# A ring of their own for the norms' small tiles, and 32-byte steps between operand slots, in a hybrid streaming block on one core

## The chip, the cores and the metric

The kernel runs on one core of a Trainium2 chip. The metric is the device time of one execution in microseconds (us); for the kernel before it is 1710.43 us, the median of three runs (1708.87 to 1712.0).

A core has a matrix engine (TensorE, PE; its weight loads appear as a row of their own, PEld), VectorE (DVE), ScalarE (ACT) and GpSimd (POOL), each of which works through its own list of instructions in order, and DMA queues that SyncE (SP), ACT or POOL issue to.

## The reference

One layer takes x (1024 frames of 1024 channels) and 256 memory tokens. Everything is float32.

```python
h = _rmsnorm(x, norm_mix_g[l])
z = h @ w_in[l]
(hq, hf, hi, hg, fq, fk, fv, ff, mq, gate_logits) = jnp.split(z, pts, axis=-1)
y_a = _hgrn2_mixer(hq, hf, hi, hg, lower_bounds[l], hgrn_norm_g[l])
y_b = _fox_mixer(fq, fk, fv, ff, fox_f_bias[l], fox_q_norm_g[l], fox_k_norm_g[l])
mem_kv = _rmsnorm(mem, norm_mem_g[l]) @ mem_kv_w[l]
y_c = _memory_mixer(mq, mem_kv, mem_q_norm_g[l], mem_k_norm_g[l])
gates = jax.nn.sigmoid(gate_logits).reshape(B, T, N_BRANCH, D_MODEL)
merged = sum over branches of gates[:, :, b] * (y_b @ w_br_b)
x = x + merged @ w_out[l]
h2 = _rmsnorm(x, norm_ffn_g[l])
x = x + _conv_glu_ffn(h2, ffn_w_up[l], ffn_conv_w[l], ffn_conv_b[l], ffn_w_down[l])
```

(The two lines on the branches are drawn together here.) The memory mixer normalises its queries and keys per head, takes a softmax over the 256 tokens for each of four heads, and sums the values. The forgetting attention (FoX) normalises its queries and keys per head of 64 channels too. `_rmsnorm` divides by the root of the mean square. Such a division per head is what the kernel calls a head norm.

## The kernel before, in words

**Products.** Each float32 operand is kept as a high and a low part, and `mm3` (lines 122 to 124) makes a product of three matmuls: high by high, high by low, low by high. The large products use seven products of sums of blocks in place of eight (a Strassen-like scheme). The blocks of x are the *families* B11, B21, T2, T1, T3, B22 and T4, each with a high and a low tile of 8 KB per partition in the pool `pfam`; the weights' parts are split on the fly into the slots `wh` and `wl`. A family or slot is read again and again by PE.

**Stages.** By the time of the trace: up to 40 us the memory's keys and values and the loading of x; to 305 us the dense stage, in five units (0: memory queries, 1: HGRN's values, 2: FoX queries and keys of the first half, 3: FoX values, 4: FoX queries and keys of the second half); to 960 us the gates, HGRN, FoX and the branches; to 1070 us the out projection; to 1490 us the way up; then the way down. A unit of the dense stage (`tm_unit`) makes its seven products one after the other, each in two banks of PSUM (`pp`, `lg` or `po`), and hands each finished quarter to a `put` function.

**The head norm** (`head_norm`, lines 601 to 612) is called for the quarters of units 0, 2 and 4: ACT squares the quarter into the two banks of a product (L608), DVE sums the squares per head into a small tile `r` (L609), `rstd_small` scales it on DVE (L140) and raises it to the power of -1/2 on POOL (L141), and DVE multiplies the quarter `e` by it (L612). PE then turns the quarter with an identity into the same two banks (L617), from where ACT and DVE split it. Until that is done, these two banks cannot take a later product; the next unit's first product, with B11, needs the pair of unit 2's second norm.

**The memory attention** (`mem_attn`) is woven into the dense stage: eight times a load and twice two steps. *Logits*: six matmuls, DVE's maximum (L667) into a small tile `mst`, its negation (L668), exponentials on ACT (L670), the reciprocal on DVE (L672), the scaling on POOL (L674). *Values*: four turnings on PE (L682), the split of the result into `mph` on ACT (L128) and `mpl` on DVE (L136), six matmuls, and a copy on ACT (L690). Each step's PSUM tile is one of the two `tr` banks. `stage` takes three such steps from the list after each product of a unit.

**Small tiles.** `small` hands out slots of one ring of eight, 64 bytes per partition each. Both `r` of a head norm (named `r2` or `r4`) and `mst` come from it, in the order in which the program allocates them. A new tile of a ring waits for the tile that had its slot before.

**The order of the work** on each engine is not written out by hand: the program is emitted in the order of the code, and a scheduler that simulates the engines picks from it, at build time, the order that each engine's list gets. Which tile waits for which slot is part of what it reckons with. The chip then runs these lists as they stand.

**Addresses.** Tiles are placed one after the other in their pools. `EDGE` and `BASE` are the lengths (in floats) of two unused tiles ahead of the others on the two sides of the memory. Before the change, all families and all slots of the weights' parts start at a multiple of 128 bytes.

Of the kernel before, what the change touches and what calls it, by code (L numbers as in the profile page):

```python
# [9 lines left out]
F32 = mybir.dt.float32  # L10
F32R = mybir.dt.float32r
# [4 lines left out]
P = 128  # L16
T = 1024
D = 1024
KC = D // P
HB = 512  # L20
# [16 lines left out]
UNITS = [[("f", 0), ("q", 0)], [("g", 0), ("f", 1)], [("q", 1), ("g", 1)], [("f", 2), ("q", 2)],  # L37
         [("g", 2), ("f", 3)], [("q", 3), ("g", 3)]]
UNITS += [[("gt", i), ("gt", i + 1)] for i in range(0, 24, 2)]
EDGE, BASE = 120, 56  # L40
TMIN, TMAX = -(1.0 - 2.0 ** -24), 1.0 - 2.0 ** -23


# [26 lines left out]
def tile_block(ctx: ExitStack, tc: tile.TileContext, xT, x_rows, memT, mem_rows, vec, fbias, mats, hmask, w_ff, w_tm, w_cm,  # L70
# [4 lines left out]
    cp = ctx.enter_context(tc.tile_pool(name="cp", bufs=1))  # L75
# [22 lines left out]
    lbm, lbe0, lbe1 = (cp.tile([P, 4], F32, tag=t, name=t) for t in ("lbm", "lbe0", "lbe1"))  # L98

    def small(name, w):  # L100
        return cp.tile([P, 16], F32, tag="small", name=name, bufs=8)[:, :w]

    edge = ctx.enter_context(tc.tile_pool(name="edge", bufs=1, side="right"))
    edge.tile([P, EDGE], F32, tag="edge", name="edge")
# [2 lines left out]
    def col(i):  # L107
        return cv[:, i:i + 1]
# [29 lines left out]
    def rstd_small(out, ss, n):  # L138
        w = ss.shape[1]
        V.tensor_scalar(out, ss, 1.0 / n, EPS, ALU.mult, ALU.add)  # L140
        return G.tensor_tensor(out, out, mhalf[:, :w], ALU.pow)  # L141
# [23 lines left out]
    pfam = tc.alloc_tile_pool(name="pfam", bufs=1, side="right", reuse_waits="tile")  # L165
    fam = {}

    def fam_tile(name, part, shape=(P, 4, HB), dt=F32R):
        return pfam.tile(list(shape), dt, tag=f"{name}{part}", name=f"{name}{part}")

    rp = tc.alloc_tile_pool(name="rp", bufs=1, side="left", reuse_waits="tile")
    xp = tc.alloc_tile_pool(name="xp", bufs=1, side="left", reuse_waits="tile")
    for name in ("B11", "B21"):
        fam[name] = [fam_tile(name, p) for p in "hl"]

    def raw_tile(name="raw"):
# [3 lines left out]
        return rp.tile([P, T], dt, tag="ws", name=name, bufs=2)  # L180

    def parts_tiles():
        return [rp.tile([P, T], F32R, tag=t, name=t, bufs=3) for t in ("wh", "wl")]

    def e_tile(name="e"):
        return rp.tile([P, 4, 256], F32, tag="e", name=name, bufs=3)
# [1 line left out]
    def ko_tile(name="ko", dt=F32R):  # L188
        return rp.tile([P, 2, HB], dt, tag="ko", name=name, bufs=2)

    xr = [fam_tile(f, p, (P, 2, T), F32) for f in ("T2", "T1") for p in "hl"]
    mt = fam_tile("T3", "h", (P, KC, NM), F32)
    mem_row = fam_tile("T3", "l", (P, 2, T), F32)
    umh = fam_tile("T4", "h", (P, KC, NM))
    uml = fam_tile("T4", "l", (P, KC, NM))
    xq = [[xp.tile([P, 4, HB], F32, tag=f"x{c}{n}", name=f"x{c}{n}") for n in range(2)] for c in range(2)]
# [85 lines left out]
    def kv_chunk(q):  # L282

        ps = pairs[2 * (q // 4)]
        h, l = parts_tiles()
        for i in range(2 if q == 0 else 1):
            sl = slice(i * HB, (i + 1) * HB) if q == 0 else slice(0, T)
            split(S, h[:, sl], l[:, sl], wkv[q][:, sl])
        h, l = (t.rearrange("p (a b) -> p a b", a=2) for t in (h, l))
        for kk in range(2):  # L290
            k = 2 * (q % 4) + kk
            for m in range(2):
                ms = slice(m * P, (m + 1) * P)
                mm3(ps[m], umh[:, k, ms], uml[:, k, ms], h[:, kk, :], l[:, kk, :], k == 0, k == KC - 1)
# [49 lines left out]
    def quarter(c, n, k):  # L344
        return xq[c][n][:, k, :]

    def turn_x(c, n, k):
        ps = ps_tr()
        for b in range(4):
            PE.transpose(ps[:, b * P:(b + 1) * P], x_row(4 * n + b)[:, (4 * c + k) * P:(4 * c + k + 1) * P], ident)  # L350
        S.activation(quarter(c, n, k), ps, AF.Copy, scale=col(C_GX + 4 * c + k))
# [10 lines left out]
    def new_family(name):  # L362
        fam[name] = [fam_tile(name, p) for p in "hl"]

    def family_block(name, k, src, sub=None):
        h, l = fam[name]
        split(S, h[:, k, :], l[:, k, :], src, sub)
# [30 lines left out]

    def second_half():
        fam["B12"] = [fam_tile("T4", p) for p in "hl"]  # L400
        new_family("B22")
        for c, name in enumerate(("B12", "B22")):
            for k in range(4):
                turn_x(c, 1, k)
                family_block(name, k, quarter(c, 1, k))
# [30 lines left out]
    def tm_operand(src):  # L436
        h, l = parts_tiles()
        split(S, h, l, src)
        return [t.rearrange("p (k c) -> p k c", k=4) for t in (h, l)]
# [129 lines left out]
    def forget_row():  # L569
        fb = small("fb", 2)[:16, :]  # L570
        V.memset(fb, 0.0)
        a, b = (half_tile(f"fr{i}")[:16, :] for i in range(2))
        for n in range(2):
            SP.dma_start(fb[8 * n:8 * n + 8, 0:1], fbias)
            SP.dma_start(a[8 * n:8 * n + 8, :], ffd[:, n * HB:(n + 1) * HB])
        V.tensor_scalar(a, a, fb[:, 0:1], None, ALU.add)
        S.activation(b, a, AF.Abs)
        S.activation(b, b, AF.Sigmoid)
        S.activation(b, b, AF.Ln)
        V.scalar_tensor_tensor(out=b, in0=a, scalar=0.0, in1=b, op0=ALU.min, op1=ALU.add)  # L580
        V.tensor_tensor_scan(a, ones[:16, :].to_broadcast([16, HB]), b, 0.0, ALU.mult, ALU.subtract)
        SP.dma_start(fb[8:16, 1:2], a[0:8, HB - 1:HB])
        V.tensor_scalar(a, a, fb[:, 1:2], None, ALU.add)
        for n in range(2):
            SP.dma_start(negFd[:, n * HB:(n + 1) * HB], a[8 * n:8 * n + 8, :])
# [15 lines left out]
    def head_norm(z, nh, bank):  # L601

        zz = [z[:, 2 * b:2 * b + 2, :].rearrange("p b (h d) -> p (b h) d", h=nh) for b in range(2)]
        r = small(f"r{nh}", 4 * nh)
        rs = [r[:, 2 * nh * b:2 * nh * (b + 1)] for b in range(2)]
        for b in range(2):
            sq = bank[b].rearrange("p (c d) -> p c d", c=2 * nh)
            S.activation(sq, zz[b], AF.Square)  # L608
            V.reduce_sum(rs[b], sq, axis=AX.X)  # L609
        rstd_small(r, r, 256 // nh)  # L610
        for b in range(2):
            V.tensor_mul(zz[b], zz[b], rs[b].unsqueeze(2).to_broadcast([P, 2 * nh, 256 // nh]))  # L612
# [37 lines left out]
    def mem_attn(h, n):  # L650
# [8 lines left out]
        def logits(j):  # L659
            mqh, mql = tiles  # L660
            ps = ps_tr()
            pt = half_tile("mpt").rearrange("p (b m) -> p b m", b=2)
            st = small("mst", 8)
            for b in range(2):
                tsl = slice((2 * j + b) * P, (2 * j + b + 1) * P)
                mm3(ps[:, b * NM:(b + 1) * NM], mqh[:, tsl], mql[:, tsl], mem["mkh"][:, h, :], mem["mkl"][:, h, :], True, True)
            V.reduce_max(st[:, 0:2], ps.rearrange("p (b m) -> p b m", b=2), axis=AX.X)  # L667
            V.tensor_scalar(st[:, 2:4], st[:, 0:2], -1.0, None, ALU.mult)  # L668
            for b in range(2):
                S.activation(pt[:, b, :], ps[:, b * NM:(b + 1) * NM], AF.Exp, bias=st[:, 2 + b:3 + b],  # L670
                             accum_out=st[:, 4 + b:5 + b])
            V.reciprocal(st[:, 6:8], st[:, 4:6])  # L672
            for b in range(2):
                G.tensor_scalar(pt[:, b, :], pt[:, b, :], st[:, 6 + b:7 + b], 0.0, ALU.mult, ALU.add)  # L674
            pts.append(pt)
# [26 lines left out]
    def mem_steps():  # L702
# [9 lines left out]
        slow.extend(steps)  # L712

    stage(0, put_mq, (None, second_half, None, differences, mem_keys, third))
    small_consts()
    stage(1, put_hi, (last, mem_steps, forget_logits, forget_row))
# [513 lines left out]
    wp = tc.alloc_tile_pool(name="wp", bufs=1, side="left", reuse_waits="tile")  # L1230
    pr = tc.alloc_tile_pool(name="pr", bufs=1, side="right", reuse_waits="tile")
    r2 = pr.tile([P, T], F32, tag="r2", name="r2")
    pl = tc.alloc_tile_pool(name="pl", bufs=1, side="right", reuse_waits="tile")
# [8 lines left out]
        return wp.tile([P, 2, HB], F32, tag="raw", name=name, bufs=4)  # L1242

    def part_tiles(bufs=4):
        return [wp.tile([P, 2, HB], F32R, tag=t, name=t, bufs=bufs) for t in ("wh", "wl")]

    def w_operand(src):
        parts = []
# [93 lines left out]
            G.dma_start(b11, b21, accum_op=ALU.add)  # L1342

    def operand_parts(h, src):
        l = pl.tile([P, HB], F32R, tag="wl2", name="wl2", bufs=5)
        late["cast"] = S.copy(h, src)  # L1346
        late["split"] = V.tensor_sub(l, src, h.bitcast(F32))  # L1347
        return h, l

    def first_operands(a11, s1, s2, s4):  # L1350

        (h0, _), (h1, _) = part_tiles(), part_tiles()
        o1 = operand_parts(h0[:, 0, :], a11)
        o2 = operand_parts(h0[:, 1, :], s1)
        o3 = operand_parts(h1[:, 0, :], s2)
        return o1, o2, o3, operand_parts(pl.tile([P, HB], F32R, tag="wl2", name="wh2", bufs=5), s4)

    with tc.issue_after(marks["last"].ins):
        run_all(up_sums())
# [9 lines left out]
    for i, (c, n, mine, first, sign, last) in enumerate((  # L1369
# [11 lines left out]
        if i < 6:  # L1381
            ops.append(operands(i + 1))
        else:
            begun = first_operands(*first_raw)
# [53 lines left out]
    pw = tc.alloc_tile_pool(name="pw", bufs=1, side="left", reuse_waits="tile")  # L1438

    def operand(src):  # L1440
        return operand_parts(pw.tile([P, HB], F32R, tag="wh2", name="wh2", bufs=6), src)

    def sum_of(i, a, b):
        t = pw.tile([P, HB], F32, tag=f"s{i}", name=f"s{i}")
# [99 lines left out]
    for p in range(NF // 2):  # L1544
# [32 lines left out]
        for i in range(2):  # L1577
            f = 2 * p + i
            c = pq.tile([P, T], F32, tag="fc", name="fc", bufs=4)
            w = [col(C_CW + t * NF + f) for t in range(3)]  # L1580
# [88 lines left out]
    for a, b, own, first, c, n, sign, last, xq in (  # L1669
# [9 lines left out]
        for i, ks in enumerate(steps):  # L1679
# [11 lines left out]
            for m in range(4):  # L1691
                w = 256 if end and ks.stop == NP and m == 3 else HB
# [115 lines left out]
```

## Time and profile before

| | |
|---|---|
| median of three runs | 1710.43 us (1708.87 to 1712.0) |
| the profiled execution's own time | 1705.72 us |
| its span in the trace | 1704.0 us |
| instructions | 24944 |
| PE busy | 1660.5 us, 97% of the span |
| DVE, ACT, POOL busy | 1211.0, 844.3, 452.7 us |
| moved by DMA | 305.54 MB |

Rows of a stage (view of windows) give its bounds in us, its length, and then for each engine the busy time and the number of instructions (x), the granted clock of PE as a share of full speed, the DMA engines' mean busy share, and GB/s. Rows of the timeline give the start, the duration, engine, line, operation and tiles (out<-in); what stands in brackets is the idle time just before and what ended it. Rows of waits give the engine, what it was about to do, what it waited for, the total, the number of times and the longest. Rows of groups give the busy time and the mean duration in ns, then the idle time ahead of them.

### The profile page before, as it was taken

What the parts mean: (1) busy time and instruction counts of PE and PEld (TensorE: products, weight loads), DVE (VectorE), ACT (ScalarE), POOL (GpSimd) and SP (SyncE); (2) the same over time, 40 slices, a digit from 0 to 9 for tenths busy, and PEclk for the clock granted to TensorE, in tenths of its full rate; (3) what the DMA queues carried; (4) which work ended last, traced back from release to release, by engine and by line L of the source; (5) the groups of instructions that cost most, each with busy time, mean ns of one, the idle gap of its engine ahead of it and who ended that gap; (6) DMA issues with size and microseconds to landing.
All of it is one profiled execution on the core that took longest, in us unless ns stands there. A gap on an engine that the chain in (4) does not pass through costs nothing. (4 is left out here: it accounts for less than half of the span.)

```text
span 1704.0 us, 24944 instructions
## 1 busy us (share of the span) xinstructions
PE 1660.5 (97%) x8883; PEld 1417.7 (83%) x8883; DVE 1211.0 (71%) x2177; ACT 844.3 (50%) x1449; POOL 452.7 (27%) x482
## 2 busy tenths in 40 slices
PE   7999989999999999999999999999999999999999
PEld 5989979977788888888888788788888888888887
DVE  7874565668787676698766767787778878765654
ACT  7745544456666666556432356643434434343432
POOL 1433344365544444323011133311111111100000
PEclk9999989999999999999999999999999999999999
DMA  7352343365564444455966998866445445394772
GB/s 288 110 187 96 108 136 147 125 200 167 174 192 138 146 141 148 161 167 191 317 194 174 300 264 207 227 177 172 153 134 140 118 146 152 117 397 158 246 272 87
DMA packets 134749, 305.54 MB, mean 179 GB/s; under 512 B 14328, under 2 KB 31992, under 8 KB 133984
## 3 DMA queue, kind: packets, MB, share of 16 engines
q1 hardware_dynamic: 101008, 210.87, 36.5%
q0 software_dynamic: 24400, 78.39, 18.3%
q10 hardware_dynamic: 9216, 14.68, 2.3%
q8 instruction: 70, 1.15, 0.3%
q14 instruction: 55, 0.45, 0.1%
HBM read 223.21 MB, written 107.41 MB: 194 GB/s over the span
## 5 line engine op out<-in xcount | busy, mean ns | idle before, releaser
L1346 ACT CAST wh<-s 128x512 fp32r<-128x512 f32 x80 | 48.8, 619 | 113.2 <-PE pp L123 61.1
L128 ACT CAST dwh<-wr 128x1024 fp32r<-128x1024 f32 (+1 forms) x41 | 40.2, 980 | 115.7 <-PE tr L123 39.2
L730 ACT CAST uh<-ur 128x512 fp32r<-128x512 f32 x78 | 48.2, 618 | 77.5 <-PE pp L123 70.9
L1346 ACT CAST wh<-rw 128x512 fp32r<-128x512 f32 x70 | 43.0, 620 | 84.0 <-PE pp L123 45.5
L1470 POOL DMA_DIRECT2D rw<-in_w_up x40 | 22.3, 567 | 188.4 <-DVE wl L1347 142.4
L1045 POOL TENSOR_SCALAR pt<-pt,st 128x128 f32<-128x128 f32 (+3 forms) x64 | 56.8, 889 | 56.8 <-DVE st L1044 38.2
L136 DVE TENSOR_TENSOR dwl<-wr,dwh 128x1024 fp32r<-128x1024 f32 (+1 forms) x41 | 46.3, 1129 | 34.1 <-ACT dwh L128 33.3
L122 PE MATMUL pp<-B21h,uh 128*128 128x512 f32 x168 | 66.8, 400 | 3.8 <-DVE gt L895 2.6
L731 DVE TENSOR_TENSOR ul<-us,uh 128x512 fp32r<-128x512 f32 x72 | 55.2, 770 | 20.1 <-ACT uh L730 19.5
L1043 ACT ACTIVATE pt<-pt,st 128x128 f32<-128x128 f32 (+3 forms) x64 | 49.8, 778 | 39.1 <-DVE st L1040 33.6
L736 POOL TENSOR_TENSOR us<-ur 128x512 f32<-128x512 f32 x36 | 48.6, 1351 | 71.5 <-DMA ur<-in_w_cm 55.4
L731 DVE TENSOR_TENSOR ul<-ur,uh 128x512 fp32r<-128x512 f32 x78 | 60.8, 779 | 8.8 <-ACT uh L730 8.3
L124 PE MATMUL pp<-B21h,ul 128*128 128x512 f32 x168 | 66.3, 394 | 0.1
L123 PE MATMUL pp<-T2l,uh 128*128 128x512 f32 x168 | 66.3, 395 | 0.0
L122 PE MATMUL pp<-T2h,uh 128*128 128x512 f32 x168 | 66.2, 397 | 0.0
L123 PE MATMUL pp<-B21l,uh 128*128 128x512 f32 x168 | 66.0, 393 | 0.0
L124 PE MATMUL pp<-T2h,ul 128*128 128x512 f32 x168 | 65.9, 393 | 0.0
L736 POOL TENSOR_TENSOR us<-us,ur 128x512 f32<-128x512 f32 x36 | 50.7, 1409 | 38.1 <-issue 31.9
L730 ACT CAST uh<-us 128x512 fp32r<-128x512 f32 x72 | 43.9, 615 | 33.7 <-POOL us L736 17.9
L1347 DVE TENSOR_TENSOR wl<-rw,wh 128x512 fp32r<-128x512 f32 x70 | 47.0, 685 | 17.7 <-PE pp L124 14.9
L136 DVE TENSOR_TENSOR wl<-raw,wh 128x1024 fp32r<-128x1024 f32 x29 | 36.8, 1273 | 27.7 <-ACT wh L128 27.5
L1347 DVE TENSOR_TENSOR wl<-s,wh 128x512 fp32r<-128x512 f32 x80 | 54.5, 681 | 0.0
(721 smaller groups left out, 6157.6 us busy)
## 6 DMA issues: line engine op xcount, KB each, us to landing
rw<-in_w_up POOLq DMA_DIRECT2D x40, 512.0 KB, 4.8
ur<-in_w_cm SPq DMA_DIRECT2D x72, 256.0 KB, 3.5
sd<-in_w_dn POOLq DMA_DIRECT2D x30, 512.0 KB, 6.1
br<-yd SPq DMA_DIRECT2D x30, 512.0 KB, 4.6
gd<-uo ACTq DMA_DIRECT2D x48, 256.0 KB, 2.2
gt<-gd SPq DMA_DIRECT2D x48, 256.0 KB, 7.5
yd<-fc SPq DMA_DIRECT2D x44, 256.0 KB, 2.0
raw<-in_w_tm SPq DMA_DIRECT2D x20, 512.0 KB, 3.4
```

Of the source, the lines that this page charges most:

```text
L122: PE.matmul(ps, lh, rh, start=first, stop=False, skip_group_check=more)
L123: PE.matmul(ps, lh, rl, start=False, stop=False, skip_group_check=more)
L124: return PE.matmul(ps, ll, rh, start=False, stop=last, skip_group_check=more)
L128: S.copy(out, in_)
L136: return (sub or V).tensor_sub(l, src, h.bitcast(F32))
L730: marks["cast"] = S.copy(h, src)
L731: V.tensor_sub(l, src, h.bitcast(F32))
L736: G.tensor_add(t, a, b)
L1043: S.activation(pt[:, :ns], pt[:, :ns], AF.Exp, bias=st[:, 2:3], accum_out=st[:, 3:4])
L1045: G.tensor_scalar(pt[:, :ns], pt[:, :ns], st[:, 3:4], 0.0, ALU.mult, ALU.add)
L1346: late["cast"] = S.copy(h, src)
L1347: late["split"] = V.tensor_sub(l, src, h.bitcast(F32))
```

## The change

It has two parts.

*Two rings.* The slots of `small` shrink from 64 to 32 bytes, still eight of them; `head_norm` takes its `r` from a new ring, `norm`, with four slots of 64 bytes. Together they take the same 512 bytes.

*Addresses.* Unused tiles of 32 bytes (`gap`) go ahead of the families B21, T2, T1, T3, T4 and B22, and the first unused tile on that side (`EDGE`) is 256 bytes shorter. The slots `wh`/`wl` of the dense stage and of the out projection and `wl2`/`wh2` of the way up become 32 bytes longer than what is used of them, so that the slots of one ring stand 32 bytes further apart. By the addresses of the built kernels, the families start after the change at 64 (B11), 96 (B21), 0 (T2), 32 (T1), 64 (T3), 96 (T4) and 0 (B22) within 128 bytes; the dense stage's `wh` at 0, 32 and 64 and its `wl` at 96, 0 and 32; those of the out projection and the way up in like steps of 32. The gates' slots `uh` and `ul` all move to 64. The way down's slots stay at multiples of 128.

```diff
-EDGE, BASE = 120, 56
+EDGE, BASE = 56, 56
...
     def small(name, w):
-        return cp.tile([P, 16], F32, tag="small", name=name, bufs=8)[:, :w]
+        return cp.tile([P, 8], F32, tag="small", name=name, bufs=8)[:, :w]
...
+    def gap(name):
+        pfam.tile([P, 8], F32, tag=f"gap{name}", name=f"gap{name}")
+
     for name in ("B11", "B21"):
+        if name == "B21":
+            gap(name)
         fam[name] = [fam_tile(name, p) for p in "hl"]
...
-        return [rp.tile([P, T], F32R, tag=t, name=t, bufs=3) for t in ("wh", "wl")]
+        return [rp.tile([P, T + 8], F32R, tag=t, name=t, bufs=3)[:, :T] for t in ("wh", "wl")]
...
-    xr = [fam_tile(f, p, (P, 2, T), F32) for f in ("T2", "T1") for p in "hl"]
+    xr = []
+    for f in ("T2", "T1"):
+        gap(f)
+        xr += [fam_tile(f, p, (P, 2, T), F32) for p in "hl"]
+    gap("T3")
...
+    gap("T4")
...
         fam["B12"] = [fam_tile("T4", p) for p in "hl"]
+        gap("B22")
         new_family("B22")
...
     def head_norm(z, nh, bank):
...
-        r = small(f"r{nh}", 4 * nh)
+        r = cp.tile([P, 16], F32, tag="norm", name=f"r{nh}", bufs=4)[:, :4 * nh]
...
     def part_tiles(bufs=4):
-        return [wp.tile([P, 2, HB], F32R, tag=t, name=t, bufs=bufs) for t in ("wh", "wl")]
+        return [wp.tile([P, T + 8], F32R, tag=t, name=t, bufs=bufs)[:, :T].rearrange("p (a b) -> p a b", a=2) for t in ("wh", "wl")]
...
     def operand_parts(h, src):
-        l = pl.tile([P, HB], F32R, tag="wl2", name="wl2", bufs=5)
+        l = pl.tile([P, HB + 8], F32R, tag="wl2", name="wl2", bufs=5)[:, :HB]
```

(`wh2` is lengthened in the same way at its two places.) Lines behind the first added ones have numbers higher by up to 12 in the kernel after: L609 becomes L621, L612 L624, L617 L629, L667 L679, L674 L686, L682 L694.

The number of instructions of each engine stays the same. Their order changes in the units 2 to 4 of the dense stage alone.

On DVE, around the second head norm of unit 2, the order before is this (`e_2307` is the quarter, `r4_2423` its small tile, `mst` the small tiles of the attention; the numbers tell one tile from another):

```order
L667 TENSOR_REDUCE mst_2359<-tr_2357 128x2
L609 TENSOR_REDUCE r4_2423<-pp_201 128x8
L609 TENSOR_REDUCE r4_2423<-pp_202 128x8
L668 TENSOR_SCALAR mst_2359<-mst_2359 128x2
L136 TENSOR_TENSOR mpl_2462<-tr_2456,mph_2461 128x512
L140 TENSOR_SCALAR r4_2423<-r4_2423 128x16
L672 RECIPROCAL mst_2359<-mst_2359 128x2
L612 TENSOR_TENSOR e_2307<-e_2307,r4_2423 128x512 x2
```

And after the change, where the same quarter is `e_2313` and its small tile `r4_2429`:

```order
L148 SCALAR_TENSOR_TENSOR e_2313<-lg_210,e_2313 128x512
L684 RECIPROCAL mst_1883<-mst_1883 128x2
L621 TENSOR_REDUCE r4_2429<-pp_206 128x8
L148 SCALAR_TENSOR_TENSOR e_2313<-lg_211,e_2313 128x512
L136 TENSOR_TENSOR wl_2724<-raw_2323,wh_2723 128x1024
L621 TENSOR_REDUCE r4_2429<-pp_207 128x8
L140 TENSOR_SCALAR r4_2429<-r4_2429 128x16
```

The sums of the norm have moved forward to the combine that makes the quarter (L148). The `mst` that stood ahead of them before is the one allocated just ahead of `r4`; after the change its reduce stands 51 rows behind the first sum, and another, earlier one (`mst_1883`) is being worked on here.

On PE, the turning of this quarter (L617) stands before the change among the matmuls of the attention (`mkh`, `mkl` with `mqh`, `mql` are logits; `mpt` is being turned, and `mph`, `mpl` with `mvh`, `mvl` are values):

```order
L124 MATMUL tr_2492<-mkh_1264,mql_2454 128x256
L617 MATMUL pp_201<-ident_73,e_2307 128x128 x2
L617 MATMUL pp_202<-ident_73,e_2307 128x128 x2
L682 MATMUL tr_2474<-ident_73,mpt_2358 128x128 x3
L617 MATMUL pp_201<-ident_73,e_2307 128x128 x2
L617 MATMUL pp_202<-ident_73,e_2307 128x128 x2
L122 MATMUL tr_2474<-mph_2479,mvh_1266 128x256
```

After the change it stands in the middle of unit 2's last product, the one with T4:

```order
L122 MATMUL lg_210<-wh_2573,T4h_1201 128x256
L123 MATMUL lg_210<-wl_2574,T4h_1201 128x256
L124 MATMUL lg_210<-wh_2573,T4l_1202 128x256
L694 MATMUL tr_2117<-ident_73,mpt_2003 128x128 x3
L629 MATMUL pp_206<-ident_73,e_2313 128x128 x2
L629 MATMUL pp_207<-ident_73,e_2313 128x128 x2
L629 MATMUL pp_206<-ident_73,e_2313 128x128 x2
L629 MATMUL pp_207<-ident_73,e_2313 128x128 x2
L122 MATMUL lg_211<-wh_2573,T4h_1201 128x256
```

Before, 12 more matmuls of the attention follow and then unit 3's first product (`pp_201` with B11), and the last product of unit 2 has ended some 100 PE instructions of attention and turning ahead of it. After, the rest of the product with T4 and six matmuls of the attention follow, and then unit 3's first product (`pp_206` with B11); the attention that stood here is spread over the products of units 3 and 4.

More of the change, by code (lines that the diff above doesn't have):

```diff
@@ L1355, in first_operands @@
         o3 = operand_parts(h1[:, 0, :], s2)
-        return o1, o2, o3, operand_parts(pl.tile([P, HB], F32R, tag="wl2", name="wh2", bufs=5), s4)
+        return o1, o2, o3, operand_parts(pl.tile([P, HB + 8], F32R, tag="wl2", name="wh2", bufs=5)[:, :HB], s4)
     with tc.issue_after(marks["last"].ins):
@@ L1440, in operand @@
     def operand(src):
-        return operand_parts(pw.tile([P, HB], F32R, tag="wh2", name="wh2", bufs=6), src)
+        return operand_parts(pw.tile([P, HB + 8], F32R, tag="wh2", name="wh2", bufs=6)[:, :HB], src)
     def sum_of(i, a, b):
```

## The prediction

> **What bounds the kernel now.** I read the page first, then the busy time stage by stage, then what TensorE (PE) waits for, and last the order of time inside the one stage that stands out. The page:
>
> ```profile
> span 1704.0 us, 24944 instructions
> PE 1660.5 (97%) x8883; PEld 1417.7 (83%) x8883; DVE 1211.0 (71%) x2177; ACT 844.3 (50%) x1449; POOL 452.7 (27%) x482
> ...
> PE   7999989999999999999999999999999999999999
> ...
> PEclk9999989999999999999999999999999999999999
> ```
>
> PE is the bound: 97% busy, and only the first and the sixth slice (213 to 256 us) fall below nine tenths; in the sixth the granted clock drops too. So two things can move the time: what leaves PE idle, and how long one matmul takes. The stages:
>
> ```profile
> core 0: us, PE busy (x) PEld busy (x) DVE busy (x) ACT busy (x) POOL busy (x), PEclk, DMA share, GB/s
> 40.00:172.00 132.00, 130.03 (x1042) 124.63 (x1041) 89.61 (x137) 76.01 (x139) 50.67 (x34) 1.00 0.40 134
> 172.00:200.00 28.00, 28.00 (x237) 28.00 (x236) 14.64 (x25) 12.89 (x29) 10.88 (x10) 1.00 0.26 90
> 206.45:235.14 28.69, 16.70 (x93) 14.23 (x92) 15.11 (x33) 14.62 (x40) 9.87 (x10) 0.82 0.23 79
> 235.14:305.00 69.86, 69.86 (x588) 69.86 (x587) 41.45 (x53) 32.57 (x52) 29.70 (x21) 1.00 0.44 162
> 305.00:960.00 655.00, 644.90 (x3505) 546.12 (x3504) 482.66 (x1141) 355.86 (x686) 243.04 (x251) 0.99 0.57 181
> 960.00:1070.00 110.00, 105.26 (x466) 86.28 (x464) 76.51 (x100) 63.42 (x93) 31.80 (x38) 1.00 0.96 248
> 1070.00:1490.00 420.00, 419.09 (x1854) 347.39 (x1855) 333.09 (x497) 179.31 (x273) 68.10 (x108) 1.00 0.53 152
> 1100.00:1450.00 350.00, 350.00 (x1546) 289.91 (x1545) 281.03 (x420) 144.50 (x221) 49.24 (x78) 1.00 0.54 153
> ```
>
> From 206.45 to 235.14 us PE does 93 matmuls, where the next stage does 588 in 69.86 us, 0.1188 us each. At that pace the 93 take 93 x 0.1188 = 11.05 us, so 28.69 - 11.05 = 17.64 us are lost: idle, and matmuls drawn out at a clock of 0.82. It is one hole at the border of dense units 2 and 3; the stages around it are full. What PE waits for in it:
>
> ```profile
> engine line waited for: us in total, times, longest us
> PE tr L122 <- DVE mpl L136: 4.9, 5, 1.8
> PE tr L682 <- POOL mpt L674: 3.0, 1, 3.0
> PE tr L122 <- ACT yo L690: 1.9, 1, 1.9
> PE tr L122 <- ACT mpt L670: 1.9, 2, 1.0
> ```
>
> All four are steps of the memory attention that wait for each other. That names what PE was doing, not why it had nothing else: unit 3's product lay ready. Four engines in order of time give the why:
>
> ```profile
> 210.01 0.64 ACT L608 ACTIVATE pp<-e 128x512 f32<-128x512 f32 x1
> ...
> 222.22 0.69 DVE L667 TENSOR_REDUCE mst<-tr 128x2 f32<-128x512 f32 x1 [0.86 <-PE tr L124]
> 222.83 1.28 DVE L609 TENSOR_REDUCE r<-pp 128x8 f32<-128x512 f32 x2
> ...
> 224.70 0.16 DVE L140 TENSOR_SCALAR r<-r 128x16 f32<-128x16 f32 x1
> ...
> 227.88 1.49 DVE L612 TENSOR_TENSOR e<-e,r 128x512 f32<-128x512 f32 x2 [2.38 <-POOL r L141]
> ...
> 224.94 2.91 POOL L141 TENSOR_TENSOR r<-r,mhalf 128x16 f32<-128x16 f32 x1 [2.55 <-DVE r L140]
> ...
> 230.45 1.05 PE L617 MATMUL pp<-ident,e 128*128 128x128 f32 x4
> ...
> 235.14 0.28 PE L122 MATMUL pp<-wh,B11h 128*128 128x256 f32 x1
> ```
>
> The second head norm of unit 2 has its squares by 210.01 + 0.64 = 210.65 us. DVE sums them only at 222.83, 12.2 us later, right behind the reduce of an attention step (222.22): in DVE's order the sum stands behind that step, and the step hangs on PE's attention chain. Then come the power on POOL, the scaling (227.88) and the turning (230.45), and only then are the two banks free that unit 3's first product needs (235.14). The chip follows this order; the norm itself is short.
>
> **The change part by part.** *The rings.* No instruction is added or taken away. In the order before, each of unit 2's four `r4` reduces stands directly behind the reduce of the `mst` that was allocated just ahead of it, as it must when both draw on one ring that gives slots out in turn. Behind the change `r4` has a ring of its own, and its reduce stands behind the combine that makes its `e`; the `mst` it used to follow comes about fifty rows of DVE later. PE's order follows: before, the turning of `e_2307` lies among 100 PE instructions of attention and turning alone, between unit 2's last product and unit 3's first; after, the same norm is turned inside the last product, six attention matmuls follow it, then unit 3's first product, and the rest of the attention lies between the products of units 3 and 4. That is how 172 to 200 us lie today, 237 matmuls in 28.00 us with PE busy for 28.00. So the hole's work stays, at 0.1188 us each, and up to 17.64 us of waiting go.
>
> What is late next? A norm's chain, from these rows:
>
> ```profile
> L608 ACT ACTIVATE pp<-e 128x512 f32<-128x512 f32 x15 | 9.1, 608 | 13.5 <-DVE e L150 9.0 <-DVE e L148 4.3
> L609 DVE TENSOR_REDUCE r<-pp 128x8 f32<-128x512 f32 x10 | 6.7, 686 | 3.3 <-ACT pp L608 3.3
> L612 DVE TENSOR_TENSOR e<-e,r 128x512 f32<-128x512 f32 x24 | 17.4, 765 | 7.2 <-POOL r L141 7.2
> L141 POOL TENSOR_TENSOR r<-r,mhalf 128x16 f32<-128x16 f32 x8 | 23.2, 2905 | 29.4 <-DVE r L140 29.3
> ```
>
> Two squares 1.2, two sums 1.4, the scalar step 0.2 (0.16 above), the power 2.9, two scalings 1.5, and two combines ahead at about a sum's length 1.4: 8.6 us. In the new order 90 to 101 rows of PE stand between the end of the product that feeds a norm and its turning, 90 x 0.1188 = 10.7 us at the least. The chain fits with 2 us over, little when DVE and ACT serve attention too. The nearest row for what is left is unit 0, where four norms of the same build meet a full PE:
>
> ```profile
> PE pp L617 <- DVE e L612: 1.3, 1, 1.3
> PE lg L617 <- DVE e L612: 0.6, 1, 0.6
> ```
>
> These 1.9 us agree with that stage's idle time, 132.00 - 130.03 = 1.97. I take 2.0 as what remains; the ends are 0 (172 to 200) and about half the hole, 9 us, if attention steps miss their places between the products. Gain: 17.64 - 2.0 = 15.6 us.
>
> *The addresses.* Families and weight parts start at different multiples of 32 bytes; before, all at multiples of 128. No order and no count depends on it. What could change is the time of one matmul. The stage 1100 to 1450 gives 350.00 / 1546 = 0.2264 us with all at multiples of 128. The trace of before has one place with 128x512 matmuls whose weights lie elsewhere: the forget logits, 32 of them, whose weights (`wf`) are 40 columns, 160 bytes, apart, so at 0, 32, 64 and 96 within 128 in turn. The first four of L560 and the last of L561:
>
> ```profile
> 122.55 0.39 PE L560 MATMUL tr<-B11h,wf 128*40 128x512 f32 x1
> ...
> 123.01 0.39 PE L560 MATMUL tr<-B11h,wf 128*40 128x512 f32 x1
> ...
> 123.47 0.39 PE L560 MATMUL tr<-B11h,wf 128*40 128x512 f32 x1
> ...
> 123.93 0.40 PE L560 MATMUL tr<-B11h,wf 128*40 128x512 f32 x1
> ...
> 129.73 0.39 PE L561 MATMUL tr<-T3l,wf 128*8 128x512 f32 x1
> ```
>
> (129.73 - 122.55) / 31 = 0.2316 us, 2.3% above the other row. But their weights have 40 and 8 columns in turn instead of 128, and the four offsets start an even 0.46 apart. So the offset shows no effect, and I take 0. From above, the 2.3% bounds it: the stages above hold 1,414 us of PE work from 40 to 1490 (130 + 28 + 17 + 70 + 645 + 105 + 419), so +33 us. From below, a matmul of 256 columns starts every 0.1188 us, so 512 columns cost 0.2264 - 0.1188 = 0.1076 us more than 256 and about 0.011 us per matmul is not columns; if that were a clash of addresses and all went, PE would gain 0.011 / 0.2264 = 4.9% of 1,414 us, 69 us. No row speaks for either. The Trainium skill, page "SBUF — State Buffer", section "Who interferes with whom", says that PE and ACT never wait on anyone for their ports, its moving operand and its weight load each having a port of their own; by that the addresses are worth 0 on PE; the forget logits' even spacing agrees, and no run here moves a family.
>
> DMAs into moved tiles are the other price. Weights of the way up land far ahead:
>
> ```profile
> rw<-in_w_up POOLq DMA_DIRECT2D x40, 512.0 KB, 4.8
> ```
>
> That is 4.8 us against a unit of 84 matmuls, 84 x 0.2264 = 19.0 us. Only the out projection is tight, DMA share 0.96 with PE idle for 110.00 - 105.26 = 4.7 us. I take 0, since PE is fed for 96% of it even so; the end is that its idle time doubles, +5 us, and below, that it goes, -5.
>
> The Trainium skill, page "DMA: Bandwidth & Descriptors", section "How a descriptor splits into AXI transactions", says that a descriptor which does not start on 256 bytes pays for the bytes from the boundary below it; this speaks against the change: for rows of 4 KB one transaction in 17 more, an estimate of 6% from that page, and by it 110 x 0.96 x 0.06 = 6 us more in the out projection, a time of 1701. No run here shows such a transfer yet.
>
> *The sum.* 17.6 - 2.0 + 0 + 0 = 15.6 us. The profiled execution took 1705.72 us around its span of 1704.0, so its like would be 1690.1; the median of the three runs is 1710.43, 4.7 above, and the hole should be the same in each: 1710.43 - 15.6 = 1694.8 us.
>
> **The rivals.**
>
> *Half of it comes back.* Attention now shares units 3 and 4 with the norms and the splits of weights; if PE waits there for `mpt`, `mpl` or `e` as it did in the hole, about 9 of the 17.6 us return: 1710.4 - 8.6 = 1701.8. For it: a margin of only 2 us in the norm's chain. Against it: 172 to 200 us without an idle moment, and DVE busy only 41.45 of 69.86 us in the stage that takes the steps over. Chance 0.12.
>
> *The out projection slows.* Transfers into moved tiles take longer where the DMAs are busy for 0.96 of the time, and PE's 4.7 us of idle time there double: 1694.8 + 5 = 1700. For it: that share. Against it: 105.26 of 110.00 us fed all the same. Chance 0.07.
>
> *The change does nothing.* The order differs but PE waits as long elsewhere in the stage, or matmuls lengthen by just what the hole gives: 1710. For it: the attention chain has the same length in either order. Against it: PE has 588 matmuls to lay beside it. Chance 0.06.
>
> *Slower: the matmul gets longer with moved operands.* Place: every product between 40 and 1490 us. Each 1% is 14 us of the 1,414. It decides from 15.6 / 1414 = 1.1%, 2.5 ns on 226, and it is slower by over 0.2% from 19.0 / 1414 = 1.34%. At the 2.3% of the forget logits it would be +33 - 15.6 = +17 us, 1728. For it: that row. Against it: there the offset itself changes nothing from one matmul to the next. Chance 0.08.
>
> *Much faster: operands that clashed no longer do.* By a third of the 69 us above, 23 more: 1672. For it, the 11 ns per matmul that are not columns; against it, that the forget logits with spread offsets are not shorter. Chance 0.05.
>
> **How the numbers follow.** The forecast has the rest, 0.62, at 1694.8. Its own range is 1688 (nothing left of the hole, and all the out projection's idle time gone: 1710.4 - 17.6 - 4.7) to 1698 (3 us more left of the hole). The slower out projection carries it to 1700, the half case, with up to 4 us more lost in the hole, to 1706. Left out are no change, slower and much faster, 0.19. With 1 us of spread at the lower end, 1687 to 1706. A measurement of this kernel can tell about 0.2%, 3.4 us, from no change; forecast, out projection, half and much faster lie beyond that: faster 0.62 + 0.07 + 0.12 + 0.05 = 0.86, same 0.06, slower 0.08.
>
> **What would show it.** Right: between unit 2's last product and unit 3's first only a microsecond instead of 29, no dip of the granted clock in the sixth slice, DVE's sum for the second norm within 2 us of its square, the stages behind it as long as now but some 15 us earlier, and 0.2264 us per matmul in the way up. Wrong: new idle rows of PE for `mpt`, `mpl` or `e` in units 3 and 4 (half), another time per matmul in 1100 to 1450 shifted by the gain (addresses), or an out projection longer than 110 us (transfers).

## The result and the profile after

The changed kernel takes 1704.26 us (median of six runs, 1702.82 to 1709.31), the kernel before 1710.98 us in the same comparison. The ratio is 0.9967, with a 95% interval from 0.9952 to 0.9983: faster by 0.3%, some 6.7 us. Forecast were 1694.8 us and a gain of 15.6 us. The time lies inside the forecast's range of 1687 to 1706 and the sign is right, but of the 15.6 us only 6.7 came.

The page of the changed kernel, the lines shown of before:

```profile
span 1702.3 us, 24935 instructions
PE 1671.0 (98%) x8883; PEld 1413.8 (83%) x8883; DVE 1212.1 (71%) x2177; ACT 844.0 (50%) x1449; POOL 455.3 (27%) x482
...
PE   8999999999999999999999999999999999999999
...
PEclk9999999999999999999999999999999999999999
```

The dip in the sixth slice is gone, in PE's busy time and in its clock. Yet PE is busy for 10.5 us more than before (1671.0 against 1660.5), with the same 8883 matmuls. Where the hole was, the changed kernel's timeline of PE (start, duration, operation) shows unit 2's last product, a gap of six attention matmuls, and unit 3's first product:

```profile
204.85 0.29 PE L124 MATMUL lg<-wh,T4l 128*128 128x256 f32 x1
...
205.68 0.28 PE L122 MATMUL pp<-wh,B11h 128*128 128x256 f32 x1
```

That is 0.83 us where the kernel before needed 29, and the norm's sum follows its square at once, as forecast:

```profile
187.76 0.60 ACT L620 ACTIVATE pp<-e 128x512 f32<-128x512 f32 x1
...
188.40 0.69 DVE L621 TENSOR_REDUCE r<-pp 128x8 f32<-128x512 f32 x1 [0.33 <-ACT pp L620]
```

The stages of the changed kernel, in the same bounds as before:

```profile
core 0: us, PE busy (x) PEld busy (x) DVE busy (x) ACT busy (x) POOL busy (x), PEclk, DMA share, GB/s
206.45:235.14 28.69, 28.34 (x241) 28.13 (x241) 19.43 (x32) 16.04 (x36) 13.81 (x13) 1.00 0.70 237
235.14:305.00 69.86, 69.86 (x581) 69.25 (x580) 43.62 (x61) 33.44 (x62) 28.25 (x20) 1.00 0.29 105
960.00:1070.00 110.00, 107.02 (x468) 87.32 (x467) 71.83 (x97) 65.35 (x100) 38.12 (x45) 0.97 0.92 218
1070.00:1490.00 420.00, 420.00 (x1812) 340.05 (x1811) 325.44 (x483) 172.56 (x259) 59.96 (x97) 1.00 0.51 149
...
1100.00:1450.00 350.00, 350.00 (x1510) 283.28 (x1509) 273.88 (x409) 141.92 (x216) 47.47 (x76) 1.00 0.51 147
```

241 matmuls now stand where 93 stood. But the last row has 1510 matmuls in 350 us of a full PE, where the kernel before had 1546: 350 / 1510 = 0.2318 us each in place of 0.2264. The prediction had named this row as a sign of being wrong. (The view counts the matmuls that touch the window, two more than start in it: from start to start the distances are 232.0 and 226.7 ns.)

The gates' first product and the way down's first, by the ranges "first to last start" of two tiles, in the kernel before and the kernel after:

```profile
L122 PE MATMUL pp<-B11h,uh x72: 389/389/497, 321.6 to 799.6; 128*128 128x512 f32 x72
...
L122 PE MATMUL po<-dbh,dwh x42: 389/389/397, 1495.3 to 1692.6; 128*128 128x512 f32 x42
```

```profile
L122 PE MATMUL pp<-B11h,uh x72: 387/390/499, 301.6 to 782.0; 128*128 128x512 f32 x72
...
L122 PE MATMUL po<-dbh,dwh x42: 387/389/397, 1493.7 to 1690.9; 128*128 128x512 f32 x42
```

The dense stage ends 20.0 us earlier (321.6 to 301.6). At the way down 1.6 us of that are left (1495.3 to 1493.7): the stages between take 1192.1 us where they took 1173.7, 18.4 more. (The profiled execution of before, 1705.72 us, is one of its quick ones, and the rings alone, below, take 1177.1 us for the same stretch with every operand where it was; so some 3 of the 18.4 us are that execution's luck.)

### The profile page after: what moved, and what is told of

Its sections match the earlier page's. It is cut to its first block, busy times and chain, and to the rows that moved or that the text cites. A ratio compares the mean times of both kernels' runs of the same rounds, so it can differ in the third digit from the quotient of the medians.

```text
span 1702.3 us, 24935 instructions
## 1 busy us (share of the span) xinstructions
PE 1671.0 (98%) x8883; PEld 1413.8 (83%) x8883; DVE 1212.1 (71%) x2177; ACT 844.0 (50%) x1449; POOL 455.3 (27%) x482
```

## The experiments

The theory after the result, A: the two rings gain what was forecast or more, and the addresses take most of it back, by a longer matmul. The rival, B: the rings gain only the 7 us measured, because PE waits elsewhere, and the longer matmuls cost nothing that matters.

The times of all runs first (the kernel before had medians of 1709.5 to 1711.9 us beside them; ratios are to those, and a difference of 2 us between two rows can be nothing more than that spread). "Gates" is the start of the gates' first product, "256" and "512" are the mean distance in ns between the starts of neighbouring matmuls of 256 columns in the dense stage (those under 150 ns apart) and of 512 columns in the way up (350 us by the view's count between 1100 and 1450 us).

| kernel | median us | ratio to before, 95% | gates | 256 | 512 |
|---|---|---|---|---|---|
| before | 1710.98 | | 321.6 | 119.8 | 226.4 |
| after | 1704.26 | 0.9952 to 0.9983 | 301.6 | 118.3 | 231.8 |
| e1_rings | 1691.73 | 0.9874 to 0.9900 | 303.9 | 119.9 | 226.4 |
| e2_addr | 1722.38 | 1.0051 to 1.0085 | 319.3 | 118.2 | 231.8 |
| e3_fam | 1705.90 | 0.9950 to 0.9978 | 303.5 | 118.1 | 231.8 |
| e4_slots | 1698.85 | 0.9915 to 0.9939 | 302.7 | 118.1 | 232.1 |
| e5_steps | 1700.49 | 0.9925 to 0.9960 | 305.3 | 119.9 | 231.2 |
| e6_dense | 1689.06 | 0.9857 to 0.9887 | 300.7 | 118.1 | 226.4 |
| e7_all32 | 1706.28 | 0.9966 to 0.9993 | 302.6 | 118.4 | 232.9 |
| e8_all64 | 1694.37 | 0.9883 to 0.9920 | 296.2 | 114.7 | 229.5 |
| e9_dense64 | 1685.38 | 0.9832 to 0.9874 | 299.5 | 117.2 | 226.4 |
| e10_ring12 | 1710.36 | 0.9981 to 1.0008 | 321.2 | 119.8 | 226.4 |
| e11_step128 | 1701.65 | 0.9914 to 0.9960 | 306.2 | 119.9 | 231.2 |
| e12_all256 | 1685.32 | 0.9833 to 0.9870 | 301.8 | 115.1 | 226.4 |

### The two parts alone

`e1_rings` has the rings and no other address:

```diff
-        return cp.tile([P, 16], F32, tag="small", name=name, bufs=8)[:, :w]
+        return cp.tile([P, 8], F32, tag="small", name=name, bufs=8)[:, :w]
...
-        r = small(f"r{nh}", 4 * nh)
+        r = cp.tile([P, 16], F32, tag="norm", name=f"r{nh}", bufs=4)[:, :4 * nh]
```

> The two rings alone, every operand at its old address. Theory A (the rings give what was predicted and the addresses take most of it back, through a matmul that takes 0.232 us in place of 0.2264): about 1695 us, 9 less than the changed kernel, the hole at 206 us gone and 0.2264 us per matmul from 1100 to 1450. Theory B (the rings are worth only the 7 us that were measured, since PE waits elsewhere, and the longer matmuls cost nothing that matters): about 1704 us.

`e2_addr` is the changed kernel with these two edits undone:

> The addresses alone, with the old ring of small tiles. Theory A: the hole stays and the matmuls take 0.232 us: 1711 + 9 = 1720 us. Theory B: 1711 us, no difference.

Measured: the rings alone 1691.73 us, 19.5 less than before (17 to 22 by the interval); the addresses alone 1722.38 us, 11.1 more. Both lie near what A expects, 1695 and 1720, and B is refuted: 1704 and 1711 were its numbers. In their traces PE, DVE, ACT and POOL of the rings alone do the same work in the same order as in the changed kernel, and those of the addresses alone as in the kernel before; so each pair differs by the addresses and nothing else. The parts add up: -19.5 + 11.1 = -8.4, against -6.7 for both together. The rows of the rings alone, gates, way down and the way up's stage:

```profile
L122 PE MATMUL pp<-B11h,uh x72: 387/389/497, 303.9 to 782.1; 128*128 128x512 f32 x72
...
L122 PE MATMUL po<-dbh,dwh x42: 389/389/393, 1481.0 to 1678.2; 128*128 128x512 f32 x42
...
1100.00:1450.00 350.00, 350.00 (x1546) 289.81 (x1545) 274.72 (x410) 143.38 (x220) 47.47 (x76) 1.00 0.51 146
```

The dense stage ends at 303.9 in place of 321.6: 17.7 us, the whole of the hole (17.64 in the prediction). From the gates to the way down it takes 1177.1 us; the changed kernel takes 1192.1, 15.0 more, and its dense stage 2.3 less, together 12.7 us, about what lies between the two medians (1704.26 - 1691.73 = 12.5).

### Which slots, which families

`e3_fam` keeps the rings and the families' gaps, with the slots as long as before; `e4_slots` keeps the rings and the longer slots, with `EDGE` at 120 and no gaps:

```diff
-        return [rp.tile([P, T + 8], F32R, tag=t, name=t, bufs=3)[:, :T] for t in ("wh", "wl")]
+        return [rp.tile([P, T], F32R, tag=t, name=t, bufs=3) for t in ("wh", "wl")]
...
-EDGE, BASE = 56, 56
+EDGE, BASE = 120, 56
...
-        pfam.tile([P, 8], F32, tag=f"gap{name}", name=f"gap{name}")
+        return
```

(The first pair is `e3_fam`'s, with the same in the out projection and the way up; the others are `e4_slots`'s.)

> The rings, and of the addresses the families' gaps only; the slots of the weights' parts stand side by side as before. If moved families lengthen the matmuls (theory A, whichever operand is moved): 1704 us and 0.232 us per matmul in the way up. If it is the spread slots of one ring that do it (theory A, slots): 1695 us and 0.2264 us. Theory B: 1704 us with 0.2264 us per matmul.

> The rings, and of the addresses the lengthened slots only; the families stay at multiples of 128 bytes. If any moved operand lengthens the matmuls: 1704 us and 0.232 us per matmul in the way up. If it is the families that do it: 1695 us and 0.2264 us. If it needs both operands of a matmul at different offsets: also 1704 us here, since these weights differ from their families.

The families alone cost all of it (1705.90), the slots alone half (1698.85). In the way up either is enough, 231.8 and 232.1 ns, and both together are no worse than one. The gates tell them apart. There no slot was spread, and `e4_slots` has the old 229 ns between matmuls of 512 columns, `e3_fam` and the changed kernel 232 (means of the starts from 300 to 940 us). So a stream of matmuls loses its rhythm when some of its operands lie elsewhere, and every matmul of the stream pays, also one whose own two operands kept their places: in the changed kernel's way up, those with both at a multiple of 128 come 231.7 ns after the one before as well.

### What "elsewhere" is

Four runs vary the distance. `e5_steps` and `e11_step128` put the way up's slots 64 and 128 bytes further apart, `e7_all32`, `e8_all64` and `e12_all256` move the whole side on which the families lie; all have the rings.

```diff
-        l = pl.tile([P, HB], F32R, tag="wl2", name="wl2", bufs=5)
+        l = pl.tile([P, HB + 16], F32R, tag="wl2", name="wl2", bufs=5)[:, :HB]
```

```diff
-EDGE, BASE = 120, 56
+EDGE, BASE = 112, 56
```

(16 becomes 32 in `e11_step128`; 112 becomes 104 in `e8_all64` and 56 in `e12_all256`.)

> The rings, all families at multiples of 128 bytes, and the slots of the way up alone 64 bytes further apart, so that its weights lie at 0 and 64 in turn. If what matters is the address within 64 bytes: 0.2267 us per matmul in the way up, 1692 us like the rings alone. If it is the address within 128 bytes: about 0.232 us there, some 1,850 matmuls times 5.3 ns = 10 us more than the rings alone, 1701 us. Every other stage as with the rings alone.

> The rings, and all families and every other tile on their side of the memory moved by the same 32 bytes, so that no two of them stand apart by anything but multiples of 128. If it is the address itself that counts: gates, way up and way down at 232 ns, about 1692 + 20 = 1712 us. If it is that operands differ from each other: the gates, whose weights move along, stay at 229 ns and only stages that take an operand from the other side lengthen (way up and way down), about 1706 us.

> As the run with everything on that side moved by 32 bytes, but by 64. If what matters is the address within 64 bytes: every stage as with the rings alone, 1692 us. If it is within 128 bytes: the same times as the run with 32 bytes.

> The rings, and the slots of the way up alone 128 bytes further apart, so that their spacing changes and their address within 128 does not. If the address within 128 bytes is what lengthens the matmul: 0.2267 us in the way up and 1692 us, the same as the rings alone. If it is the spacing or the place itself: 0.232 us and 1701 us, as with steps of 64.

> The rings; every tile of the families' side moved by the same 256 bytes (out projection, way up and way down then take one operand from each side); and the dense stage's weights put 64 bytes below the families' offset instead of above it. Steps of 128 bytes had broken the rhythm of the way up, so the address within 128 is not what counts; within 256 or 512 is open. If it is within 256: 226.7 ns in out projection, way up and way down as with the rings alone. If it is within 512: about 230 ns in these three stages, some 3,200 matmuls times 3.3 ns = 11 us more. In the dense stage, the order of the two offsets: if their side counts, 114.5 ns per matmul of 256 columns and 1684 us (or 1695 with the rhythm broken); if only their distance counts, 117 ns and 1685 us (or 1696).

Steps of 64 bytes cost about what steps of 32 do, 231.2 ns in the way up and 1700.49 us. That left the address within 128 bytes, and this fell with the next run: steps of 128 cost the same, 1701.65 us where 1692 were expected. (The matmuls whose own operands agree pay too, but less: 229.6 ns there, against 233.2 for those whose operands lie 128 bytes apart.) In the kernel before, all operands of the large products agree modulo 512 even, so 256 and 512 were open, and the last run settles that: with the families, and the slots that lie on their side, moved by 256 bytes against the other side, the way up keeps its rhythm. The way up of steps of 128, and of the side moved by 256:

```profile
1100.00:1450.00 350.00, 350.00 (x1514) 284.63 (x1513) 274.80 (x410) 141.50 (x216) 47.47 (x77) 1.00 0.51 147
```

```profile
1100.00:1450.00 350.00, 350.00 (x1546) 289.82 (x1545) 274.58 (x410) 144.03 (x220) 47.47 (x76) 1.00 0.50 145
```

And it is the difference between operands, not the address. With one side moved by 32, the gates, whose weights moved along with the families, keep 229 ns, while the way up goes to 232.9 and the way down, which stayed in rhythm in every kernel until then, goes from 226 to 231 ns (150 us by 663 and by 650 matmuls):

```profile
1500.00:1650.00 150.00, 150.00 (x650) 122.01 (x650) 90.37 (x93) 55.19 (x59) 0.00 (x0) 1.00 0.74 257
```

```profile
1500.00:1650.00 150.00, 150.00 (x663) 124.23 (x662) 97.57 (x99) 58.67 (x63) 0.00 (x0) 1.00 0.71 243
```

(The first is the side moved by 32, the second by 256.) The second of the two answers of that run's expectation holds, at 1706.28 us. The side moved by 64 fits neither of its answers: the gates keep 229 ns and the way up goes only half the way, to 229.5, so the loss depends on the distance; and its dense stage was the quickest of all, which led to the next runs.

### The dense stage

Matmuls of 256 columns went the other way in every run: shorter with operands apart. `e6_dense` spreads the dense stage's slots alone; `e9_dense64` puts them all 64 bytes above the families' offset; `e12_all256` has them 64 bytes below it, as `e8_all64` has. (In the dense stage the weights' parts are the moving operand, the one that streams through PE, and the family is the one loaded as weights.)

```diff
+    rp.tile([P, 16], F32, tag="pad", name="pad")
+
     def parts_tiles():
-        return [rp.tile([P, T], F32R, tag=t, name=t, bufs=3) for t in ("wh", "wl")]
+        return [rp.tile([P, T + 8], F32R, tag=t, name=t, bufs=3)[:, :T] for t in ("wh", "wl")]
```

(The pad is `e9_dense64`'s, 48 floats long in `e12_all256`; the longer slot is `e6_dense`'s.)

> The rings, and the slots of the dense stage alone 32 bytes further apart. In the runs so far a matmul of 256 columns took 118.2 ns where any operand of the dense stage was moved and 119.9 where none was. If that is worth its time: some 2,100 matmuls times 1.7 ns = 3.5 us less than the rings alone, 1688 us, with 226.7 ns from the out projection on. If the dense stage is held by the splits of the weights instead: 1692 us, the same as the rings alone.

> The rings, and one unused tile of 64 bytes ahead of the dense stage's slots, so that all its weights lie at 64 within 128 and its families at 0; nothing else moves. With everything of the other side at 64 and the weights at 0, a matmul of 256 columns had taken 114.7 ns in place of 119.9 and the dense stage had ended 7.7 us earlier than with the rings alone. If the distance of 64 between the two operands does that: the same here, 1692 - 8 = 1684 us, and every later stage as with the rings alone. If it was the families' own address: 119.9 ns and 1692 us.

`e6_dense` gives 1689.06 us, 2.7 less than the rings alone, near the 3.5 expected, but their intervals overlap. `e9_dense64` gives 1685.38, better than both kernels and 6.4 us below the rings alone, where 8 were expected: 117.2 ns, not 114.7, and the gates start at 299.5 and not at 296.2. The side counts: 64 bytes below gives 115.1 ns. But that run is no faster, 1685.32 us, and its dense stage no shorter: from the first product with B11 (44.0 and 41.7 us) to the gates (301.8 and 299.5) it is 257.8 us in both. That is not a floor: at the same side and nearly the same distance between matmuls, `e8_all64` does the stage in 254.1 us (42.0 to 296.2), where the rings alone take 262.0. In `e12_all256` PE waits longer for the quarters of the head norms (`e`), 2.3 and 1.3 us at its two longest such waits, against 1.4 and 1.2 in `e8_all64` and 1.3 and 0.8 in `e9_dense64`. That is part of the difference; the rest was not traced.

### What made the hole

`e10_ring12` is the kernel before with a shared ring of twelve slots:

```diff
-        return cp.tile([P, 16], F32, tag="small", name=name, bufs=8)[:, :w]
+        return cp.tile([P, 16], F32, tag="small", name=name, bufs=12)[:, :w]
...
-EDGE, BASE = 120, 56
+EDGE, BASE = 56, 56
```

> The kernel before with one shared ring of twelve slots in place of eight (the 256 bytes are taken from the first unused tile on the other side, so that every operand keeps its address within 128). If the hole came from too few slots: it goes, and about 1692 us. If it came from the turns, the norm's tile standing behind the attention's in one ring whatever its length: the hole stays, and 1711 us like the kernel before.

It takes 1710.36 us, DVE's list, as built, is in the same order as before, and the hole is there (206.45 to 235.14 us):

```profile
206.45:235.14 28.69, 16.80 (x93) 14.49 (x94) 15.20 (x32) 14.31 (x40) 10.19 (x10) 0.82 0.24 80
```

So it was not a lack of slots, up to twelve at least, but the sharing: in one ring the norm's tile takes its turn behind the attention's, and with a ring of its own (`e1_rings`) the hole is gone.

## Why the prediction was right and wrong

*The hole* was right in place, cause and size. The sum stood behind an attention step only because both drew on one ring; with a ring of its own it goes, and the dense stage ends 17.7 us earlier in the profile where 17.64 was the most to be had. (By the medians the rings gain 19.5 us; the 1.9 us beyond the hole are not accounted for.)

*The residue of 2.0 us* did not appear; the end taken at 0 (172 to 200 us as the model) was the right one. A small miss to the safe side.

*The addresses, taken at 0,* is the step that failed. They cost 12.5 us, by the medians of the changed kernel and of the rings alone. The row that told it was in the prediction: the forget logits at 0.2316 us against 0.2264. It was set aside because "the four offsets start an even 0.46 apart. So the offset shows no effect". But that compares matmuls within one mixed stream, and in such a stream all pay, as `e3_fam` and `e4_slots` show. The comparison to make was between that stream and one with all operands at one offset, and this gave 231.6 against 226.4, which is what the changed kernel has in the way up (231.8). The other reason given, the widths of 40 and 8 columns, was a guess with no row behind it; no run separates the widths from the offsets in that stream, so that the offsets make its 231.6 ns is likely and not shown.

The rival with this mechanism had a chance of 0.08 and 33 us. Its mechanism was right and its size was not: 2.3% of all 1,414 us. The way up pays in full (231.8 for 226.4). The gates had no full rhythm to lose (see the last section) and go from 229 to 232 ns. The dense stage gains by 1.3%. So it costs 12.5 us, which the rings' gain outweighs, and the end is a faster kernel all the same. *Much faster*, the rival in which operands that clashed no longer do, has the sign right for the matmuls of 256 columns alone: the dense stage gains 2.3 us of the 23 that it named. The rule of the Trainium skill that PE never waits on anyone for its ports ("SBUF — State Buffer", "Who interferes with whom") was read as a price of 0 on PE; the measured 12.5 us decides against that reading. The runs show no second engine that PE waits for; they show only that its matmuls come at longer distances.

*The transfers:* from 960 to 1070 us PE is busy for 107.0 of 110 us, 105.3 before and 104.5 with the rings alone; its idle time did not double. (The changed kernel and the rings alone reach the out projection some 17 us earlier than the kernel before, so it is with the rings alone that this row compares like with like.) A share of the cost in DMAs was not measured by itself, but the longer matmuls leave nothing to explain, neither 5 us of idle time nor the 6 us that the prediction estimated beside it: by their numbers they account for 9.8 us in the way up (1,824 by 5.35 ns), 6.4 in the gates (2,088 by 3.1) and 1.8 in the out projection and behind it (360 by 5.0), 18 us together, where 15.0 are lost from the gates to the way down.

*Half of it comes back* gave a time near the measured one (1701.8) by luck: its reason was wrong. Nothing came back in the dense stage, which ends 20.0 us earlier, and PE's largest wait in the changed kernel is outside it, for the gates:

```profile
PE pp L122 <- DVE gt L907: 3.3, 1, 3.3
```

## What to carry to other kernels

A change of two parts that ends a little faster can be one large gain and one large loss: time each part alone before keeping it. If the same matmuls take longer between starts, compare whole streams with each other and not the members of one stream. Small tiles of two chains that must not wait for each other belong in rings of their own; a longer shared ring, twelve slots in place of eight, did not help here.

## What the runs showed of the hardware

Matmuls of 512 columns in a full stream start 226.7 ns apart when all operands of the stream have the same address modulo 256 bytes: in the way up of the kernel before, every distance is 226 or 227 ns. With operands 32 bytes apart they scatter, mostly between 226 and 238 ns, 232 in the mean; steps of 64 and 128 bytes give 231, and one side moved by 64 as a whole gives 229.5. The rhythm has to be found: with the rings alone, the first matmuls after a wait come further apart and then fall into 0.227 us. A timeline of that kernel in the gates stage:

```profile
804.49 0.40 PE L123 MATMUL pp<-T4l,uh 128*128 128x512 f32 x1
...
806.36 0.40 PE L122 MATMUL pp<-T4h,uh 128*128 128x512 f32 x1
...
806.82 0.39 PE L124 MATMUL pp<-T4h,ul 128*128 128x512 f32 x1
...
808.41 0.39 PE L124 MATMUL pp<-T2h,ul 128*128 128x512 f32 x1
```

Ten steps from 804.49 to 806.82 in 2.33 us, 0.233 each, then seven in 1.59, 0.227 each. Over the gates stage of that kernel, the first four distances after an interruption (a distance of 250 ns or more, or a matmul of another shape) have a mean of 231.3 ns, those from the twelfth on 226.7; in the changed kernel the latter have 231.6. The gates are interrupted so often that the kernel before has 229 there.

Matmuls of 256 columns behave the other way: 119.9 ns with all operands at one offset, 118 with them spread, 115 when the moving operand lies 64 bytes below the other (modulo 256; 114.7 and 115.1 in two kernels), 117 when it lies 64 above. At 64 below, most distances are 113 or 114 ns, half of 226.7. Why operands at one offset shorten the distance at 512 columns and lengthen it at 256 stays open; no run looked inside the engine. So does what kept the dense stage of `e12_all256` 3.7 us longer than that of `e8_all64` at nearly the same distance.
